# One of five score products contracts 128 rows instead of 64: the rotary keys' low halves in two zero-padded copies

## The chip, the cores and the metric

The kernel runs on one core of a Trainium2 chip. The metric is the device time of one execution in microseconds (us). Before the change it is 720.41 us, the median of 3 runs (720.25 to 720.73).

## The reference

One decoder layer over 512 tokens of width 1024: two parallel mixers with gates, an output projection, and a gated feed-forward with a causal convolution, all float32. The change touches the attention's scores alone. Each of 8 heads has 128 features without position and 64 turned by position (the rotary part); the rotary key is one for all heads:

```
k_rope = apply_rope(k_rope, cos, sin)                      # (tokens, 64), shared by the heads
s = einsum('bqhd,bkhd->bhqk', qn, k_nope) + einsum('bqhr,bkr->bhqk', qr, k_rope)
s = where(key_pos <= q_pos, s * scale, -inf)
p = softmax(s);  out = einsum('bhqk,bkhd->bqhd', p, v)     # queries in blocks of 128
```

## The kernel before

Every float32 value that enters a product is split in two: a high part H, rounded to the format float32r, and the rest, a low part L. A product of two such values is three matmuls, H·H, H·L and L·H, summed in one bank of PSUM (`mm3`, L79). ScalarE writes H (a cast), VectorE writes L (a subtraction): the helpers `split` (L75) and `wsplit` (L65), the latter for weights.

The layer runs in stages: the norm and the small projections; the spatial gate's values (two halves `hf`, four pairs of rows `pr`); the attention, head by head; the merging of the two mixers; the output projection; the feed-forward, which is the longest. In the loop over heads (L487) each turn does, on TensorE: the scores of head h, a gate's wide projection (`gate`, 24 products of 512 columns, the bank `pza`), the transposes of head h's probabilities (`turn`, L457), the query and key projections of head h + 1 (`qk`, in every second head also `rope`, which makes the next pair's turned queries), a second wide projection (`pzu` or `pzb`), and the sum over values (`attend`, the bank `po`).

The scores of one head are four blocks of 128 queries; block i sees (i + 1) · 128 keys, so the products have 128, 256, 384 and 512 columns. Each block is five matmuls (L434 to L438): three for the part without position, two for the rotary part. For the latter `rope` keeps the queries of a pair of heads so that one tile holds both parts: the head with e = 0 has its H in partitions 0 to 63 and its L in 64 to 127, the head with e = 1 the other way round. The keys stand twice, once in each half of the partitions: `krH` (high part) and `krL` (low part), [128, 512] each. L438 contracts all 128 rows with `krH`, which gives H·H + L·H at once. L437 contracts the 64 rows `own` in which the query's H lies, with `krL`. The keys are split once, at L323, in the stage of the spatial gate's values.

The softmax of a block is on VectorE and ScalarE: mask (L440), maximum (L441), exponential (L443), reciprocal (L445), scaling (L446). The transposes of block i read what L446 wrote for it. The work of heads 0 to 3 also carries a layer norm of the spatial gate's values (L521 to L531), mostly on VectorE.

A scheduler (the tile framework) sets the order on each engine from the order of the code and from priorities; the softmax has a high one. Engines take their instructions in that order. SP's queue issues the loads of weights ahead of their use into three rotating buffers.

Of the kernel before, what the change touches and what calls it, by code (L numbers as in the profile page):

```python
# [15 lines left out]
P = 128  # L16
D = 1024
S = 512
# [14 lines left out]

# columns of the packed per-feature parameters
PM, PQ, PFF, PCW, PCB, PFN = 0, 8, 11, 19, 151, 195
NPAR = 203
# columns of the packed constants
CI, CM, CF = 0, 128, 256
# [4 lines left out]
def block_kernel(ctx, tc, xT, pos, w_s, w_v, w_g, w_q, w_kv, w_o, w_u, w_d,  # L43
# [39 lines left out]

# [1 line left out]
    part = cp.tile([P, NPAR], F32, name="part")  # L85
# [4 lines left out]

    # the scalar engine's first table
    tb = cp.tile([P, 1], F32, name="tb")
# [18 lines left out]

    # keeps the tensor engine's clock up until the first operands are there
    pw = bank("warm")
# [3 lines left out]
    def col_mean(o, terms, c):  # L117
        """o [P, blocks]: by token, the sums over partitions of the terms, times column c of mcol."""
        for b in range(o.shape[1]):
            for a, t in enumerate(terms):  # L120
                T.matmul(o[:, b:b + 1], lhsT=t[:, b * P:(b + 1) * P], rhs=mcol[:, c:c + 1],
                         start=a == 0, stop=a == len(terms) - 1)
# [5 lines left out]
    def over_partitions(rt, pool, n, cols=NT):  # L128
        """A value by token, [P, cols], on all partitions: a bank [P, cols * P]."""
        dH = pool.tile([P, cols * P], F32R, tag="dH", name=f"dH_{n}", bufs=1)  # L130
        dL = pool.tile([P, cols * P], F32R, tag="dL", name=f"dL_{n}", bufs=1)
        for b in range(cols):
            c = slice(b * P, (b + 1) * P)
            A.mul(dH[:, c], ident, rt[:, b:b + 1])
            V.scalar_tensor_tensor(out=dL[:, c], in0=ident, scalar=rt[:, b:b + 1], in1=dH[:, c].bitcast(F32),
                                   op0=ALU.mult, op1=ALU.subtract)
        pb = bank(f"pb_{n}")
        T.matmul(pb[:, :cols * P], lhsT=ones, rhs=dH, start=True, stop=False)
        T.matmul(pb[:, :cols * P], lhsT=ones, rhs=dL, start=False, stop=True)
        return pb[:, :cols * P]  # L140
# [10 lines left out]
    def turned(t1, t2, z):  # L151
        """t1: z turned by its tokens' angles; 64 features after 64, a feature's partner 32 away."""
        V.tensor_tensor(out=t1, in0=z, in1=CC, op=ALU.mult)
        for q in range(4):
            a, b = slice(32 * q, 32 * q + 32), slice(32 * (q ^ 1), 32 * (q ^ 1) + 32)
            V.tensor_tensor(out=t2[a], in0=z[b], in1=SS[b], op=ALU.mult)
        V.tensor_tensor(out=t1, in0=t1, in1=t2, op=ALU.add)

# [1 line left out]
    hH = [None] * KC  # L160
# [12 lines left out]
    krH = mx.tile([P, S], F32R, name="krH")  # L173
    krL = mx.tile([P, S], F32R, name="krL")
    cqH = [mx.tile([P, S], F32R, name=f"cqH{i}") for i in range(2)]
# [5 lines left out]
    with tc.tile_pool(name="st", bufs=2) as st:  # L181
        # x, by chunks of features; the first weights behind each pair of them
        raws = []
# [40 lines left out]

        # rotary tables, by token, then turned: the cosines [c c c c], the sines [s -s s -s]
        ang = st.tile([P, P], F32, tag="ang", name="ang", bufs=1)
# [7 lines left out]
        def turns(o, t, unit):  # L234
            """Whole turns in t, to a multiple of the unit."""
            V.tensor_scalar(out=o, in0=t, scalar1=1.0 / (TWO_PI * unit), scalar2=MAGIC, op0=ALU.mult, op1=ALU.add)
            V.tensor_scalar(out=o, in0=o, scalar1=MAGIC, scalar2=unit, op0=ALU.subtract, op1=ALU.mult)
# [3 lines left out]

        # a turn in three parts, the first two short enough for exact products
        n8 = st.tile([P, P], F32, tag="n8", name="n8", bufs=1)
# [22 lines left out]

        # low-rank queries and keys, times their norms' gains; the squares without them
        pmx = bank("pm_x")
# [11 lines left out]

        # the spatial gate's values, by token: two halves of the features, four banks each
        for hf in range(2):
            pv = [bank(f"pv{hf}{t}") for t in range(NT)]
            for pr in range(4):
# [8 lines left out]
                if hf == 0 and pr == 0:  # L293
# [3 lines left out]
                    col_mean(pmq[:, NT:2 * NT], sqs[2:], 2)  # L297
                    # rstd_x * (mean(raw^2) * rstd_x^2 + eps)^-1/2
                    msq = st.tile([P, 2, NT], F32, tag="msq", name="msq", bufs=1)
# [5 lines left out]
                    inv_root(rtq.rearrange("p a t -> p (a t)"), msq.rearrange("p a t -> p (a t)"))  # L305
                    # the queries carry the scores' scale
                    for i in range(2):
# [10 lines left out]
                if hf == 0 and pr == 2:  # L318
                    V.tensor_tensor(out=cq[3], in0=cq[3], in1=rx, op=ALU.mult)
                    t1 = st.tile([P, S], F32, tag="t1", name="kt1", bufs=1)  # L320
                    t2 = st.tile([P, S], F32, tag="t2", name="kt2", bufs=1)
                    turned(t1, t2, cq[3])
                    split(krH, krL, t1)  # L323
                if hf == 1 and pr == 0:
# [13 lines left out]
    def gchunk(n, g):  # L338
        """One chunk of 128 of the wide projection's features, over all tokens."""
        raw = wtile(w_g[g], f"g{g}")  # L340
        wh, wl = wsplit(raw, f"g{g}")
        pz = bank(f"pz{n}{g}")
        for j in range(KC):
            c = slice(j * P, (j + 1) * P)
            mm3(pz, wh[:, c], wl[:, c], hH[j], hL[j], j == 0, j == KC - 1)
        return pz
# [19 lines left out]
    with tc.tile_pool(name="at", bufs=1) as at:  # L366
# [25 lines left out]
        def qproj(o, g, c0):  # L392
            """128 columns of a pair of heads' queries, from c0 of each half of the rows."""
            wh, wl = wqs[g]
            for k in range(2):
                c = slice(k * 384 + c0, k * 384 + c0 + P)
                mm3(o, wh[:, c], wl[:, c], cqH[k], cqL[k], k == 0, k == 1)

        def rope(g):
            """A pair of heads: the turned queries' parts, [H | L] of the one and [L | H] of the other."""  # L400
            pa = bank(f"ra{g}")
# [4 lines left out]
            for e in range(2):  # L406
# [3 lines left out]
                V.tensor_tensor(out=T_[oth], in0=t1[own], in1=T_[own].bitcast(F32), op=ALU.subtract)  # L410
                rT[2 * g + e] = (T_, own)

# [11 lines left out]
        def scores(h, qt):  # L424
            qH, qL, kH, kL = qt
            tq, own = rT[h]
            p_ = at.tile([P, 1280], F32, tag="p", name=f"p{h}")
            sm = at.tile([P, 3, 4], F32, tag="sm", name=f"sm{h}", bufs=2)
            pS = [bank(f"s{h}{i}") for i in range(NT)]
            for i in range(NT):  # L430
# [5 lines left out]
                T.matmul(o, lhsT=qL[:, qs], rhs=kH[:, :n], start=False, stop=False)  # L436
                T.matmul(o, lhsT=tq[own, qs], rhs=krL[own, :n], start=False, stop=False)  # L437
                T.matmul(o, lhsT=tq[:, qs], rhs=krH[:, :n], start=False, stop=True)  # L438
# [9 lines left out]

        # turned blocks: keys 0 | keys 1, keys 3 | keys 2
        place = {0: (0, 0), 1: (1, 0), 3: (1, 384), 2: (2, 0)}  # L450
# [36 lines left out]
        for h in range(H):  # L487
# [18 lines left out]
            if h == 0:  # L506
# [3 lines left out]
                                base=0, channel_multiplier=-1)  # L510
                # layer norm of the values; their gains and shifts lie where late chunks will
                gb = [uy.tile([P, S], F32, tag=f"u{4 + i}", name=f"gb{i}") for i in range(4)]
# [21 lines left out]
    with tc.tile_pool(name="mg", bufs=2) as mg:  # L534
# [17 lines left out]

        # output projection, the residual, and the next norm's squares
        x1t = [hp.tile([P, D], F32, tag=f"d{t}", name=f"x1_{t}") for t in range(NT)]
# [21 lines left out]

# [1 line left out]
    fp = ctx.enter_context(tc.tile_pool(name="fp", bufs=1))  # L578
# [14 lines left out]
    def conv(pz, f):  # L593
        """f: the chunk's place in the parameters; a causal convolution of width three."""
        z = f2.tile([P, S + 2], F32, tag="z", name=f"z{f}")
# [39 lines left out]
    for j in range(KC - 2):  # L635
# [13 lines left out]
        if j == 1:  # L649
            # the last two chunks' weights, where the normed residual was and behind it  # L650
            eh, el = [], []
# [21 lines left out]

    # the last two chunks: three blocks of tokens as before, then the fourth by token; its other
    # features are turned to it, so that only a quarter's norm is left behind the last product
    n = S - P
# [21 lines left out]
    for i in range(NF):  # L698
        mm3(pB[:, :256], aH[i][:, tB], aL[i][:, tB], eh[i], el[i], i == 0, i == NF - 1)
        if i == 1:  # L700
            # the residual, turned as it is added
            for k in range(2):
# [29 lines left out]
def _layout(x, positions, mix_norm, w_in, a_v_norm_g, a_v_norm_b, a_spatial_w, a_spatial_b, q_a_norm,  # L732
# [11 lines left out]
    def rows(m):  # L744
        # [pairs of 128 rows, partition, (which of the pair, column)]
        return m.reshape(4, 2, P, -1).transpose(0, 2, 1, 3).reshape(4, P, -1)

    def cols(m):
        # [128 columns, partition, (chunk of 128 rows, column)]
        k, n = m.shape  # L750
# [58 lines left out]
```

## Time and profile before

| | |
|---|---|
| median of 3 runs | 720.41 us |
| profiled execution, its span from first to last instruction | 720.1 us |
| busy: TensorE products / weight loads | 710.9 us / 587.8 us |
| busy: VectorE / ScalarE / GpSimd | 476.9 us / 331.6 us / 11.4 us |
| granted TensorE clock, mean | 0.998 |
| DMA, mean over the span | 97 GB/s |

The profile gives for the profiled execution its span alone; the 0.3 us between it and the median is all that can be said of what lies around it. PE is TensorE's stream of products, PEld its weight loads, DVE is VectorE, ACT ScalarE, POOL GpSimd. Starts of matmuls are recorded, their ends are modelled, and a product's recorded duration overlaps that of the next: the time that a product takes from the stream is the distance from its start to the next one's start. Transposes are float32 products with the identity.

### The profile page before, as it was taken

What the parts mean: (1) busy time and instruction counts of PE and PEld (TensorE: products, weight loads), DVE (VectorE), ACT (ScalarE), POOL (GpSimd) and SP (SyncE); (2) the same over time, 40 slices, a digit from 0 to 9 for tenths busy, and PEclk for the clock granted to TensorE, in tenths of its full rate; (3) what the DMA queues carried; (4) which work ended last, traced back from release to release, by engine and by line L of the source; (5) the groups of instructions that cost most, each with busy time, mean ns of one, the idle gap of its engine ahead of it and who ended that gap; (6) DMA issues with size and microseconds to landing.
All of it is one profiled execution on the core that took longest, in us unless ns stands there. A gap on an engine that the chain in (4) does not pass through costs nothing.

```text
span 720.1 us, 8624 instructions
## 1 busy us (share of the span) xinstructions
PE 710.9 (99%) x3303; PEld 587.8 (82%) x3303; DVE 476.9 (66%) x816; ACT 331.6 (46%) x496; POOL 11.4 (2%) x14
## 2 busy tenths in 40 slices
PE   8999999999999999999999999999999999999996
PEld 5888877788787888878888888888888888888896
DVE  7966799967668567765477777776777775432104
ACT  5465555774756543343354444444444444422101
POOL 0000110000000000000100000000000000000000
PEclk9999999999999999999999999999999999999999
DMA  7524422130111111252322232222223225631003
GB/s 248 177 76 142 162 81 80 59 111 30 58 61 58 60 59 58 95 198 90 111 93 88 89 112 93 89 102 103 88 93 112 85 83 162 189 102 52 0 1 117
DMA packets 22617, 69.63 MB, mean 97 GB/s; under 512 B 2736, under 2 KB 4400, under 8 KB 22576
## 3 DMA queue, kind: packets, MB, share of 16 engines
q1 hardware_dynamic: 21568, 66.72, 27.6%
q10 hardware_dynamic: 1008, 2.36, 0.9%
q8 instruction: 26, 0.43, 0.3%
q14 instruction: 15, 0.12, 0.1%
HBM read 66.97 MB, written 2.10 MB: 96 GB/s over the span
## 4 chain that ended last, share of the span: by engine, by line
PE 97%; DMA 1%; SPq 0%; ACT 0%; DVE 0%; issue 0%; POOLq 0%; DVEq 0%
PE pup L80 11%; PE pup L82 11%; PE pup L81 11%; PE pd L82 4%; PE pd L81 4%; PE pd L80 4%; PE pout L81 2%; PE pout L82 2%; PE pout L80 2%; PE pv L80 2%; PE pza L82 2%; PE pzb L80 2%; PE pzb L82 2%; PE pza L80 2%; PE pzu L81 2%; PE pza L81 2%
## 5 line engine op out<-in xcount | busy, mean ns | idle before, releaser
L70 ACT CAST wh_u<-wr_u 128x1024 fp32r<-128x1024 f32 x44 | 46.3, 1052 | 41.6 <-PE pup L81 29.5
L71 DVE TENSOR_TENSOR wl_u<-wr_u,wh_u 128x1024 fp32r<-128x1024 f32 x44 | 53.9, 1225 | 8.1 <-ACT wh_u L70 7.0
L598 DVE TENSOR_TENSOR z<-pup,r 128x512 f32<-128x512 f32 x44 | 30.2, 687 | 35.1 <-PE pup L82 35.1
L80 PE MATMUL pd<-aH,wh_d 128*128 128x512 f32 x132 | 51.3, 389 | 0.0
L81 PE MATMUL pd<-aL,wh_d 128*128 128x512 f32 x132 | 51.3, 389 | 0.0
L82 PE MATMUL pd<-aH,wl_d 128*128 128x512 f32 x132 | 51.3, 389 | 0.0
L70 ACT CAST wh_g<-wr_g 128x1024 fp32r<-128x1024 f32 x24 | 25.2, 1049 | 50.4 <-issue 29.9
L71 DVE TENSOR_TENSOR wl_d<-wr_d,wh_d 128x896 fp32r<-128x896 f32 (+1 forms) x18 | 20.4, 1136 | 29.5 <-ACT wh_d L70 29.2
L76 ACT CAST aH<-y 128x512 fp32r<-128x512 f32 x22 | 13.7, 621 | 56.7 <-DVE z L597 54.2
L70 ACT CAST wh_d<-wr_d 128x896 fp32r<-128x896 f32 (+1 forms) x18 | 17.7, 982 | 44.1 <-PE pd L81 36.1
L600 ACT ACTIVATE y<-z,part 128x512 f32<-128x512 f32 x44 | 35.9, 818 | 3.4 <-DVE z L598 1.8
L71 DVE TENSOR_TENSOR wl_g<-wr_g,wh_g 128x1024 fp32r<-128x1024 f32 x24 | 29.8, 1244 | 7.2 <-ACT wh_g L70 7.1
L604 DVE SCALAR_TENSOR_TENSOR y<-z,part,y 128x512 f32<-128x512 f32 x44 | 33.0, 751 | 1.4
L602 DVE SCALAR_TENSOR_TENSOR y<-z,part,y 128x512 f32<-128x512 f32 x44 | 32.8, 747 | 0.3 <-ACT y L600 0.3
L617 ACT ACTIVATE y<-y 128x512 f32<-128x512 f32 x22 | 13.9, 632 | 36.4 <-DVE y L604 36.4
L80 PEld LDWEIGHTS pd<-aH,wh_d 128*128 128x128 f32 x132 | 24.8, 188 | 5.2
L81 PEld LDWEIGHTS pd<-aL,wh_d 128*128 128x128 f32 x132 | 24.8, 188 | 5.2
L82 PEld LDWEIGHTS pd<-aH,wl_d 128*128 128x128 f32 x132 | 24.8, 188 | 5.1
L81 PE MATMUL pout<-mL,wh_o 128*128 128x512 f32 x64 | 25.4, 397 | 0.0
L82 PE MATMUL pout<-mH,wl_o 128*128 128x512 f32 x64 | 25.3, 395 | 0.0
L80 PE MATMUL pout<-mH,wh_o 128*128 128x512 f32 x64 | 25.2, 396 | 0.0
L77 DVE TENSOR_TENSOR aL<-y,aH 128x512 fp32r<-128x512 f32 x22 | 15.2, 693 | 14.2 <-ACT aH L76 14.2
(594 smaller groups left out, 2006.2 us busy)
## 6 DMA issues: line engine op xcount, KB each, us to landing
wr_u<-in_w_u_dram SPq DMA_DIRECT2D x44, 512.0 KB, 3.3
wr_g<-in_w_g_dram SPq DMA_DIRECT2D x24, 512.0 KB, 3.3
wr_d<-in_w_d_dram SPq DMA_DIRECT2D x12, 448.0 KB, 3.3
x<-in_xT_dram SPq DMA_DIRECT2D x16, 256.0 KB, 4.4
wr_v<-in_w_v_dram SPq DMA_DIRECT2D x8, 512.0 KB, 4.4
wr_o<-in_w_o_dram SPq DMA_DIRECT2D x8, 512.0 KB, 3.3
wr_d<-in_w_d_dram SPq DMA_DIRECT2D x6, 512.0 KB, 3.5
wr_e<-in_w_e_dram SPq DMA_DIRECT2D x5, 512.0 KB, 3.6
```

Of the source, the lines that this page charges most:

```text
L70: A.copy(th[:, lo:hi], raw[:, lo:hi])
L71: V.tensor_tensor(out=tl[:, lo:hi], in0=raw[:, lo:hi], in1=th[:, lo:hi].bitcast(F32), op=ALU.subtract)
L76: A.copy(th, src)
L77: V.tensor_tensor(out=tl, in0=src, in1=th.bitcast(F32), op=ALU.subtract)
L80: T.matmul(o, lhsT=wh, rhs=xh, start=start, stop=False)
L81: T.matmul(o, lhsT=wh, rhs=xl, start=False, stop=False)
L82: T.matmul(o, lhsT=wl, rhs=xh, start=False, stop=stop)
L598: V.tensor_tensor(out=z[:, 2:], in0=pz, in1=r2, op=ALU.mult)
L600: A.activation(out=y, in_=z[:, 2:], func=AF.Identity, scale=part[:, w + 2:w + 3], bias=part[:, PCB + f:PCB + f + 1])
L602: V.scalar_tensor_tensor(out=y, in0=z[:, 1:S + 1], scalar=part[:, w + 1:w + 2], in1=y, op0=ALU.mult, op1=ALU.add)
L604: V.scalar_tensor_tensor(out=y, in0=z[:, 0:S], scalar=part[:, w:w + 1], in1=y, op0=ALU.mult, op1=ALU.add)
L617: A.activation(out=yg, in_=yg, func=AF.Silu)
```

## The change

`krL` becomes two tiles. The copy of index e holds the low parts in the half of the partitions where a head of that parity keeps its query's H, and zeros in the other half. GpSimd fills the zeros, and VectorE makes the subtraction in two halves. L437 (now L443) contracts all 128 rows with the copy of its head's parity, as L438 (now L444) does with `krH`. The rest of the difference is comments that are gone, and the slice that the dictionary `rT` no longer carries.

```
-    krL = mx.tile([P, S], F32R, name="krL")
+    krL = [mx.tile([P, S], F32R, name=f"krL{e}") for e in range(2)]
...
-                    split(krH, krL, t1)
+
+                    A.copy(krH, t1)
+                    for e in range(2):
+                        own, oth = slice(e * 64, e * 64 + 64), slice(64 - e * 64, 128 - e * 64)
+                        G.memset(krL[e][oth].bitcast(F32), 0.0)
+                        V.tensor_tensor(out=krL[e][own], in0=t1[own], in1=krH[own].bitcast(F32),
+                                        op=ALU.subtract)
...
-                rT[2 * g + e] = (T_, own)
+                rT[2 * g + e] = T_
...
-            tq, own = rT[h]
+            tq = rT[h]
...
-                T.matmul(o, lhsT=tq[own, qs], rhs=krL[own, :n], start=False, stop=False)
+                T.matmul(o, lhsT=tq[:, qs], rhs=krL[h % 2][:, :n], start=False, stop=False)
```

On TensorE, in the scores of head 1 (s is the bank of a block's scores, qt the parts of queries and keys, rT the turned queries), before:

```order
L436 MATMUL s_1099<-qt_1008,qt_1007 128x128
L437 MATMUL s_1099<-krL,rT_784 128x128
L438 MATMUL s_1099<-krH,rT_784 128x128
L434 MATMUL s_1100<-qt_1008,qt_1006 128x256
L435 MATMUL s_1100<-qt_1009,qt_1006 128x256
```

and after the change at the same place:

```order
L442 MATMUL s_1103<-qt_1012,qt_1011 128x128
L443 MATMUL s_1103<-krL_106,rT_788 128x128
L444 MATMUL s_1103<-krH,rT_788 128x128
L440 MATMUL s_1104<-qt_1012,qt_1010 128x256
L441 MATMUL s_1104<-qt_1013,qt_1010 128x256
```

Nothing has moved there: the shape shown is that of the output, line numbers are six higher, and the product with krL reads the second copy, as head 1 is odd. The whole stream of TensorE is the same in this way.

On VectorE, in the stage of the spatial gate's values (kt is the turned key, wl the low part of a weight), before:

```order
L157 TENSOR_TENSOR kt_532<-kt_532,kt_533 128x512
L135 SCALAR_TENSOR_TENSOR dL_q<-cstt,rtq,dH_q 128x128 x2
L71 TENSOR_TENSOR wl_v_648<-wr_v_645,wh_v_647 128x1024
L77 TENSOR_TENSOR krL<-kt_532,krH 128x512
L521 BN_STATS bst_1085<-vA_112 128x6
```

and after:

```order
L157 TENSOR_TENSOR kt_533<-kt_533,kt_534 128x512
L135 SCALAR_TENSOR_TENSOR dL_q<-cstt,rtq,dH_q 128x128 x2
L71 TENSOR_TENSOR wl_v_652<-wr_v_649,wh_v_651 128x1024
L328 TENSOR_TENSOR krL_105<-kt_533,krH 64x512
L328 TENSOR_TENSOR krL_106<-kt_533,krH 64x512
L527 BN_STATS bst_1089<-vA_113 128x6
```

One instruction has become two, at the same place. On GpSimd the two fills (64x512 each) stand ahead of the first power of the norm, right behind the program's start; nothing else has moved on any engine.

## Rows read from the trace of the kernel before

**Rows 1.** The page: TensorE's busy share, and the chain that ended last, by engine

```profile
PE 710.9 (99%) x3303; PEld 587.8 (82%) x3303; DVE 476.9 (66%) x816; ACT 331.6 (46%) x496; POOL 11.4 (2%) x14
...
PE 97%; DMA 1%; SPq 0%; ACT 0%; DVE 0%; issue 0%; POOLq 0%; DVEq 0%
```

**Rows 2.** Groups by shape on TensorE: count, busy us, mean ns, idle before

```profile
L438 PE MATMUL s<-krH,rT 128*128 128x512 f32 x8 | 4.0, 500 | 0.0
L437 PE MATMUL s<-krL,rT 64*128 64x512 f32 x8 | 4.0, 499 | 0.0
```

**Rows 3.** Timeline of TensorE, scores of head 1: start us, duration us, what

```profile
115.42 0.28 PE L434 MATMUL s<-qt,qt 128*128 128x128 f32 x1
...
118.56 0.39 PE L434 MATMUL s<-qt,qt 128*128 128x512 f32 x1
...
119.02 0.40 PE L436 MATMUL s<-qt,qt 128*128 128x512 f32 x1
119.35 0.50 PE L437 MATMUL s<-krL,rT 64*128 64x512 f32 x1
119.78 0.50 PE L438 MATMUL s<-krH,rT 128*128 128x512 f32 x1
120.12 0.39 PE L80 MATMUL pza<-hH0a,wh_g 128*128 128x512 f32 x1
```

**Rows 4.** Timeline of TensorE, start and end of the last head's scores

```profile
246.34 0.28 PE L434 MATMUL s<-qt,qt 128*128 128x128 f32 x1
...
251.04 0.39 PE L80 MATMUL pza<-hH0a,wh_g 128*128 128x512 f32 x1
```

**Rows 5.** Timeline of TensorE, start of head 0's sum over values

```profile
113.55 0.39 PE L80 MATMUL po<-pH,vH 128*128 128x512 f32 x1
```

**Rows 6.** Busy us (and instructions) in three stretches, then clock, DMA share, GB/s

```profile
94.60:104.90 10.30, 10.30 (x46) 7.72 (x45) 10.23 (x28) 5.26 (x11) 0.93 (x1) 1.00 0.31 103
115.40:137.40 22.00, 22.00 (x107) 17.73 (x106) 19.61 (x42) 12.66 (x23) 0.90 (x1) 1.00 0.14 47
137.40:251.10 113.70, 113.70 (x543) 90.99 (x542) 79.45 (x162) 72.25 (x126) 0.00 (x0) 1.00 0.19 64
```

**Rows 7.** Timeline of TensorE, transposes of heads 0 and 1

```profile
104.92 1.25 PE L457 MATMUL pT<-cstt,p 128*128 128x128 f32 x10
105.93 0.47 PE L80 MATMUL pq<-cqH,wqH 128*128 128x512 f32 x1
...
125.58 1.25 PE L457 MATMUL pT<-cstt,p 128*128 128x128 f32 x10
```

**Rows 8.** Timeline of VectorE, softmax of heads 0 and 1 [idle before, releaser]

```profile
103.91 0.79 DVE L446 TENSOR_SCALAR p<-p,sm 128x384 f32<-128x384 f32 x2
...
120.31 0.30 DVE L440 TENSOR_TENSOR s<-s,cstt 128x128 f32<-128x128 f32 x1 [0.47 <-PE s L438]
...
122.90 1.06 DVE L446 TENSOR_SCALAR p<-p,sm 128x256 f32<-128x256 f32 x3
```

**Rows 9.** Timeline of VectorE, the keys' split and two splits of weights

```profile
51.16 1.22 DVE L71 TENSOR_TENSOR wl_v<-wr_v,wh_v 128x1024 fp32r<-128x1024 f32 x1
52.30 0.68 DVE L77 TENSOR_TENSOR krL<-kt,krH 128x512 fp32r<-128x512 f32 x1
53.75 0.69 DVE L521 BATCH_NORM_STATS2 bst<-vA 128x6 f32<-128x512 f32 x1 [0.77 <-ACT vA L331]
...
73.57 1.72 DVE L71 TENSOR_TENSOR wl_g<-wr_g,wh_g 128x1024 fp32r<-128x1024 f32 x1 [4.17 <-ACT wh_g L70]
```

**Rows 10.** Groups by shape on VectorE: the split of the turned queries

```profile
L410 DVE TENSOR_TENSOR rT<-t,rT 64x512 fp32r<-64x512 f32 x8 | 5.5, 686 | 0.3
```

**Rows 11.** Timeline of GpSimd: a fill, the first power, the select

```profile
0.41 0.10 POOL L795 MEMSET const-uint8-127<- 128x1 uint8 x1
30.45 1.39 POOL L126 TENSOR_TENSOR rtx<-msx,mhalf 128x4 f32<-128x4 f32 x1 [29.95 <-DVE msx L125]
...
73.11 1.10 POOL L509 TENSOR_SCALAR_AFFINE_SELECT wst<-wst 128x1024 f32<-128x1024 f32 x1 [33.43 <-DMA wst<-in_ws_t_dram]
```

## The prediction

> **What bounds the kernel now.** I read the page's busy shares first, then the chain that ended last. TensorE is busy for 710.9 of 720.1 us and the chain runs over it for 97% [rows 1], so any time taken out of TensorE's own stream is a candidate for the whole kernel, unless another engine is late right there. The second view is that of the changed line's matmuls by shape: the 64-row product with krL (L437) lasts 499 ns at 512 columns, and the 128-row product with krH behind it 500 ns [rows 2]. Half the rows are no shorter. But ends of matmuls are modelled, so the third view decides: the order of starts on TensorE in one head.
>
> Read the starts of the last block of queries in head 1 [rows 3]. From L434 to L436 are two products in 119.02 − 118.56 = 0.46, that is 0.23 us for one of 512 columns. Then L436 to L437 takes 0.33, L437 to L438 0.43, and L438 to the next product 0.34. The three distances around the 64-row product are 0.10, 0.20 and 0.11 longer than the standard 0.23. The same rows give the whole of a head: the first score product starts at 115.42 and the first one after the scores at 120.12, so the 20 products (four widths, five of each) take 4.70 us. The last head shows the same, 251.04 − 246.34 = 4.70 [rows 4]. There is no idle time in these rows: the array passes from 128 rows to 64 and back to 128, and pays around that passage.
>
> What would the 20 products take with no such passage? The kernel itself holds the answer: just before these scores the attention output runs three products of each of the same four widths, all of 128 rows, from 113.55 to the first score product at 115.42 [rows 3, 5]: 1.87 us for twelve, 0.62 us for one of each width. Five of each make 5 × 0.62 = 3.12 us. So the passages cost 4.70 − 3.12 = 1.58 us in each head.
>
> **The change part by part.** (1) The krL product takes all 128 rows, with zeros opposite the query's half that must not count. Its columns stay the same, and columns are what a product's distance goes by: 0.23 for 512, 0.62 for the four widths. It reads the same stationary tile as the krH product behind it. I take the full-height product at the price of any other, and the passages are gone: 1.58 us from each of eight heads, 12.6 us on TensorE. The bounds: nothing, if what I call a passage belongs to something that stays, and 12.6.
>
> The Trainium skill, "TensorEngine Tiling (Array Packing)", section "Theoretical Speedup", speaks against padding: a contraction of 64 rows or fewer can go up to twice as fast when the array is split in rows. By that rule the half-height product was cheap and the full one adds a whole product to every block; by the rows above the time falls. The trace does not bear the rule out here, since nothing runs beside L437: its successor starts 0.43 us later, not earlier than the standard 0.23. What such a rule would give here is worked out as the last rival.
>
> (2) What of the 12.6 us reaches the end. TensorE must not run into work of VectorE that is not ready, so I looked at both in each head. In the stretch of head 0 up to its transposes VectorE is busy for 10.23 of 10.30 us [rows 6]: it follows a backlog, and nothing in it waits for TensorE, so an earlier TensorE does not make it earlier. The last scaled probabilities of head 0 (L446, two instructions shown as one) end there at 103.91 + 0.79 = 104.70; ten transposes start at 104.92 and the next product at 105.93 [rows 7, 8], so one takes 0.10 and the four that need the last block start at 104.92 + 0.60 = 105.52. They could start 0.82 us earlier, less some 0.05 for the hand-over. Head 0 thus gives about 0.77 of its 1.58 us, and waits for the rest.
>
> In head 1 VectorE still has the backlog, but it idles 0.47 us at 120.31 for that head's last scores [rows 8], which will come 0.77 + 1.58 = 2.35 us earlier; so it moves up 0.47 us. Its last probabilities then end at 122.90 + 1.06 − 0.47 = 123.49. The transposes that need them stood at 125.58 + 0.60 = 126.18 [rows 7] and move to 123.83. They keep 0.3 us, so head 1 gives all its 1.58; should the margin be gone, the loss is a few tenths. From 115.4 to 137.4 VectorE has 22.00 − 19.61 = 2.4 us to spare, and behind that it is busy for 79 of 113.7 us [rows 6], so that the six later heads give all. The sum is 0.77 + 7 × 1.58 = 11.8 us.
>
> (3) The order on TensorE is unchanged, product for product; so no bank of PSUM, weight tile or DMA on SP's queue has a new predecessor.
>
> (4) Split of the keys' low half: VectorE's one instruction of 0.68 us at 52.30 becomes two with half the partitions and the same columns. Such an instruction, that of the queries' parts, takes 686 ns [rows 10]: 0.69 us more. Behind it VectorE idles 0.77 us for ScalarE before it can go on at 53.75 [rows 9], which covers it. Without that cover it would be 0.69 us on VectorE in a stage where TensorE waits for nothing, and the waits before the backlog of head 0 would take it up.
>
> (5) Two fills with zeros, 64 x 512, on GpSimd, which now stand first in its program. The trace has no such fill; it lies between the 0.10 us of a fill of one column and the 1.10 us of the select over 128 x 1024 [rows 11], as an estimate at most 2.2 us for both. They start near 0.5 us; GpSimd's next work is at 30.45 [rows 11], and the first reader is in head 0, past 94.6. Can they hold up VectorE? A split on VectorE at 73.57, beside the select, took 1.72 us, and one of the same shape at 51.16 took 1.22 [rows 9, 11] (I read the difference as the select's doing); so a fill could cost VectorE's first constants some tenths, at most its own 1.1 us. TensorE then runs its warming products until the first weights and features, so I take nothing, and keep 0 to 1 us in the range.
>
> The terms that reach the end are −11.8 (1 and 2), 0 (3), 0 (4) and 0 (5). Against the profiled execution's own span, 720.1 us, that gives 708.3; the median of the runs shown is 0.3 above that span, which I keep for what lies around it: 708.6 us.
>
> **The rivals.**
> VectorE's backlog eats more. Heads 0 to 2 give nothing because VectorE, nearly full in 94.6 to 115.4, does not catch up: the gain is 5 × 1.58 = 7.9 us, 712.5. For it speaks 10.23 of 10.30 busy; against it the 0.47 us of idle in head 1 and the 2.4 us in the stretch behind.
>
> It does not do what it says. The long distances belong to the turned queries, whose same tile is loaded as weights twice in a row, and not to the rows: then nothing is gained and 720.4 stays. Against it: L434 and L435 read one stationary tile (qH) as well, and the distance from the one to the other and on to L436 is the standard 0.23.
>
> The half-height product was the cheap one. If the number of rows sets a product's time, the 128-row product costs a full share more, and the distances above 0.23 stay. The place is the eight heads' TensorE stream, which nothing covers; the price is one product of each width, 0.62 us a head, 8 × 0.62 = 5.0 us, 725.4. It decides if L443 of the changed kernel keeps the 0.43 and more that L437 shows. Against it stands that 499 and 500 ns are equal, and that the distance before L437, where only a 128-row product ends, is long already.
>
> **How the numbers follow.** My forecast (10 to 12.6 us less) has 0.82, the backlog rival (6 to 10 us less) 0.10, no effect 0.05, slower 0.03. The time is 708.6. The range reaches from 707.4, where all 12.6 us come through and 0.4 is left for spread, to 711.2: head 0 giving nothing (0.8), head 1 half (0.8), and 1 us for the fills. It leaves out most of the backlog rival and the last two. A change within 0.2%, 1.4 us, can't be told from none with this kernel: that is the case of no effect. Faster 0.92, same 0.05, slower 0.03.
>
> **What would show it.** In the profile after: all five score products of a block 0.23 us apart at 512 columns, and eight stretches of scores of about 3.1 us instead of 4.7; a wait of TensorE of under 1 us for the scaled probabilities in head 0, at the transposes, and none or a trace of one in head 1; VectorE's two half splits near 52 with no wait of TensorE behind them; the fills done by 3 us. I am wrong if L443 or L444 keeps a distance over 0.3, or if the waits at the transposes go on through heads 2 and 3.

## The result and the profile after

The changed kernel takes 709.86 us (median of 4 runs, 708.88 to 710.90) against 720.57 us before (4 runs, 720.25 to 720.83): a ratio of 0.9852 with a 95% interval from 0.9838 to 0.9866. It is faster by 10.7 us, inside the predicted range and 1.3 us above the predicted 708.6 us.

The page of the profile after answers to [rows 1]; TensorE is as full as before, but 11.3 us shorter, and the chain that ended last now lies on VectorE for 3%, in the stretch that ends at head 0's transposes:

```profile
span 707.6 us, 8629 instructions
PE 699.6 (99%) x3303; PEld 586.6 (83%) x3303; DVE 476.5 (67%) x817; ACT 331.5 (47%) x496; POOL 12.3 (2%) x16
PE 94%; DVE 3%; DMA 2%; issue 0%; ACT 0%; SPq 0%; POOLq 0%; DVEq 0%
```

The groups by shape on TensorE (count, busy us, mean ns, idle before) answer to [rows 2]:

```profile
L444 PE MATMUL s<-krH,rT 128*128 128x512 f32 x8 | 3.1, 393 | 0.0
L443 PE MATMUL s<-krL,rT 128*128 128x512 f32 x8 | 3.1, 387 | 0.0
```

Both products of 512 columns have lost about 110 ns of recorded duration, the 64-row one and the 128-row one behind it. What that is worth is in the timeline of the scores of head 1 (start us, duration, what), which answers to [rows 3]:

```profile
113.23 0.28 PE L440 MATMUL s<-qt,qt 128*128 128x128 f32 x1
...
113.79 0.33 PE L440 MATMUL s<-qt,qt 128*128 128x256 f32 x1
...
115.31 0.39 PE L440 MATMUL s<-qt,qt 128*128 128x512 f32 x1
...
115.77 0.40 PE L442 MATMUL s<-qt,qt 128*128 128x512 f32 x1
116.01 0.39 PE L443 MATMUL s<-krL,rT 128*128 128x512 f32 x1
116.23 0.39 PE L444 MATMUL s<-krH,rT 128*128 128x512 f32 x1
116.46 0.39 PE L80 MATMUL pza<-hH0a,wh_g 128*128 128x512 f32 x1
```

The distances around L443 are 0.24, 0.22 and 0.23 us, where they were 0.33, 0.43 and 0.34. The scores of a head take 116.46 − 113.23 = 3.23 us instead of 4.70.

The weight loads of the same block show where the time lay. TensorE's loads before (start us, duration, what, [idle before, releaser], where "issue" stands for a wait for nothing that the profile shows):

```profile
118.79 0.19 PEld L436 LDWEIGHTS s<-qt,qt 128*128 128x128 f32 x1
119.34 0.18 PEld L437 LDWEIGHTS s<-krL,rT 64*128 64x128 f32 x1 [0.37 <-issue]
119.77 0.19 PEld L438 LDWEIGHTS s<-krH,rT 128*128 128x128 f32 x1 [0.25 <-issue]
```

and after:

```profile
115.77 0.19 PEld L443 LDWEIGHTS s<-krL,rT 128*128 128x128 f32 x1
```

Between products of 128 rows a load starts ahead of its product, with the product before it: at 118.79 for L436's product at 119.02, and after the change at 115.77 for L443's product at 116.01. Where the number of rows changed, it started together with its own product, at 119.34 and 119.77 for the products at 119.35 and 119.78. Why the load is not started ahead there, no run shows.

The last head (starts on TensorE, as in [rows 4]) shows 238.49 − 235.26 = 3.23 again:

```profile
235.26 0.28 PE L440 MATMUL s<-qt,qt 128*128 128x128 f32 x1
...
238.49 0.39 PE L80 MATMUL pza<-hH0a,wh_g 128*128 128x512 f32 x1
```

Heads 0 and 1 at the transposes, on TensorE and on VectorE, answer to [rows 7, 8]:

```profile
102.28 1.71 PE L463 MATMUL pT<-cstt,p 128*128 128x128 f32 x10
103.74 0.47 PE L80 MATMUL pq<-cqH,wqH 128*128 128x512 f32 x1
...
121.92 1.25 PE L463 MATMUL pT<-cstt,p 128*128 128x128 f32 x10
122.93 0.47 PE L80 MATMUL ra<-cqH,wqH 128*128 128x512 f32 x1
```

```profile
102.48 0.80 DVE L452 TENSOR_SCALAR p<-p,sm 128x384 f32<-128x384 f32 x2
```

In head 0 the transposes start 0.50 us behind the product ahead of them (101.78), where it was 0.23, and the ten take 1.46 us from the stream instead of 1.01, because the last block is scaled only at 103.28; in head 1 they take 1.01 again. Head 0's scores started on TensorE, before and after, at

```profile
94.80 0.22 PE L434 MATMUL s<-qt,qt 128*128 128x128 f32 x1
```

```profile
93.38 0.22 PE L440 MATMUL s<-qt,qt 128*128 128x128 f32 x1
```

From there to the first score product of head 1 were 115.42 − 94.80 = 20.62 us and are now 113.23 − 93.38 = 19.85 us, 0.77 less; each later head gave between 1.46 and 1.50.

### The profile page after: what moved, and what is told of

Read it like the earlier page. It is cut to its first block, busy times and chain, and to the rows that moved or that the text cites. A ratio compares the mean times of both kernels' runs of the same rounds, so it can differ in the third digit from the quotient of the medians.

```text
span 707.6 us, 8629 instructions
## 1 busy us (share of the span) xinstructions
PE 699.6 (99%) x3303; PEld 586.6 (83%) x3303; DVE 476.5 (67%) x817; ACT 331.5 (47%) x496; POOL 12.3 (2%) x16
## 4 chain that ended last, share of the span: by engine, by line
PE 94%; DVE 3%; DMA 2%; issue 0%; ACT 0%; SPq 0%; POOLq 0%; DVEq 0%
PE pup L81 11%; PE pup L82 11%; PE pup L80 11%; PE pd L81 4%; PE pd L80 4%; PE pd L82 4%; PE pout L81 2%; PE pout L80 2%; PE pout L82 2%; PE pzb L82 2%; PE pzb L80 2%; PE pzb L81 2%; PE pv L80 2%; PE pv L82 2%; PE pza L81 2%; PE pv L81 2%
## 5 line engine op out<-in xcount | busy, mean ns | idle before, releaser
L80 PE MATMUL pd<-aH,wh_d 128*128 128x512 f32 x132 | 51.3, 389 | 0.0
L80 PEld LDWEIGHTS pd<-aH,wh_d 128*128 128x128 f32 x132 | 24.8, 188 | 5.2
L80 PE MATMUL pout<-mH,wh_o 128*128 128x512 f32 x64 | 25.2, 396 | 0.0
```

Of the source, the lines that this page charges most:

```text
L80: T.matmul(o, lhsT=wh, rhs=xh, start=start, stop=False)
```

## The experiments

All times are medians of the runs named, but for the second profile of the kernel before, which is one run; the runs of the kernel before on the same chip stand beside them. The changed kernel was run again beside most of them.

**The changed kernel again.**

> The changed kernel itself, for more runs and a second profile. In the first profile the first score product of head 0 starts at 93.38 us, 1.42 earlier than before the change, though nothing ahead of it should be faster; the eight heads then give 0.77 + 7 x 1.47 = 11.1 us. If the 1.42 us is chance of the first transfers, it comes and goes between profiles, and the mean gain stays between 10 and 12 us. If the fills on GpSimd or another part of the change moved the start for good, head 0 starts at 93.4 again. Scores of a head: 3.23 us.

709.28 us (5 runs, 708.64 to 710.17) against 720.79 us, ratio 0.9844 (0.9831 to 0.9858). Head 0 starts at 93.39, as in the first profile and as in the profiles below whose start is that of the kernel before; so the 1.42 us ahead of head 0 were not the change's doing. Unexpected was that head 0 now gives 20.62 − 19.14 = 1.48 us and not 0.77. On VectorE the profiles part at one wait, ahead of the layer norm's second multiplication. The timeline of VectorE [idle before, releaser], in the first profile after the change and in this one:

```profile
79.32 0.75 DVE L536 SCALAR_TENSOR_TENSOR vA<-vA,rv,gb 128x512 f32<-128x512 f32 x1 [1.54 <-DMA gb<-in_vb_dram]
```

```profile
78.00 0.75 DVE L536 SCALAR_TENSOR_TENSOR vA<-vA,rv,gb 128x512 f32<-128x512 f32 x1 [0.35 <-DMA gb<-in_vb_dram]
```

All that VectorE does between there and the probabilities of head 0 moves with it: the last scaling starts at 102.48 in the one and at 101.15 in the other. And this time the transposes take 1.00 us:

```profile
102.03 1.25 PE L463 MATMUL pT<-cstt,p 128*128 128x128 f32 x10
103.03 0.47 PE L80 MATMUL pq<-cqH,wqH 128*128 128x512 f32 x1
```

**Half as many passages, with the same products.** The 64-row products of neighbouring blocks are put side by side:

```
+                odd = i % 2 == 1
+                if odd:
+                    T.matmul(o, lhsT=tq[own, qs], rhs=krL[own, :n], start=True, stop=False)
...
-                T.matmul(o, lhsT=tq[own, qs], rhs=krL[own, :n], start=False, stop=False)
-                T.matmul(o, lhsT=tq[:, qs], rhs=krH[:, :n], start=False, stop=True)
+                T.matmul(o, lhsT=tq[:, qs], rhs=krH[:, :n], start=False, stop=odd)
+                if not odd:
+                    T.matmul(o, lhsT=tq[own, qs], rhs=krL[own, :n], start=False, stop=True)
```

> The kernel before with the same 64-row products, ordered so that those of blocks 0 and 1, and those of blocks 2 and 3, stand next to each other: the array goes from 128 to 64 rows and back twice in a head instead of four times. Theory (the cost is the passage): half of the 1.47 us a head goes, 0.73 x 8 = 5.9 us, about 714.6 us, scores of a head 3.9 to 4.0 us. Rival (each 64-row product carries the cost itself, wherever it stands): 4.70 us a head and 720.5 us, as before.

715.59 us (4 runs, 714.54 to 716.56) against 720.79 us, ratio 0.9926 (0.9913 to 0.9940): 5.2 us less, where 5.9 were expected. The timeline of TensorE in head 1 shows one such pair, and the end of the scores:

```profile
113.28 0.28 PE L437 MATMUL s<-qt,qt 128*128 128x128 f32 x1
...
115.35 0.34 PE L440 MATMUL s<-krH,rT 128*128 128x384 f32 x1
115.61 0.44 PE L442 MATMUL s<-krL,rT 64*128 64x384 f32 x1
115.89 0.39 PE L436 MATMUL s<-krL,rT 64*128 64x512 f32 x1
116.22 0.50 PE L437 MATMUL s<-qt,qt 128*128 128x512 f32 x1
116.56 0.39 PE L438 MATMUL s<-qt,qt 128*128 128x512 f32 x1
...
117.25 0.39 PE L80 MATMUL pza<-hH0a,wh_g 128*128 128x512 f32 x1
```

A head takes 3.97 us, 0.73 less than 4.70. The kernel has the same 64-row products as before the change, so the cost does not go with their number.

**One passage there and back in a head.** All four 64-row products first:

```
+            for i in range(NT):
+                n = (i + 1) * P
+                T.matmul(pS[i][:, :n], lhsT=tq[own, i * P:n], rhs=krL[own, :n], start=True, stop=False)
             for i in range(NT):
...
-                T.matmul(o, lhsT=tq[own, qs], rhs=krL[own, :n], start=False, stop=False)
```

> The kernel before with the four 64-row products of a head at the front of its scores, one behind the other: one passage there and back in a head. Theory (the cost is the passage): three quarters of 1.47 go, scores of a head about 3.6 us, the gain 8 x 1.1 less some 0.3 that head 0 waits for VectorE: 712.1 us. Rival (each 64-row product carries the cost itself): 4.70 us a head, 720.5 us.

711.75 us (4 runs, 711.32 to 714.05), ratio 0.9880 (0.9865 to 0.9894): 9.0 us less. The timeline of TensorE in head 1:

```profile
112.75 0.28 PE L82 MATMUL po<-pH,vL 128*128 128x128 f32 x1
112.96 0.90 PE L432 MATMUL s<-krL,rT 64*128 64x128 f32 x4
113.79 0.33 PE L437 MATMUL s<-qt,qt 128*128 128x128 f32 x1
...
116.44 0.39 PE L80 MATMUL pza<-hH0a,wh_g 128*128 128x512 f32 x1
```

3.48 us a head, from its first score product on. But here the scores begin with the 64-row products, so the way into the stretch lies ahead of that start: the last product of the sum over values is 112.96 − 112.75 = 0.21 us ahead, where it is 0.11 before a product of 128 rows (113.12 to 113.23 in the changed kernel). With these 0.10 us the head takes 3.58. From head 1 to head 2 the distance says the same, 20.92 us against 20.57 in the changed kernel. So with four, two, one and no stretches of 64 rows a head's scores take 4.70, 3.97, 3.58 and 3.23 us: 0.37 us for each stretch, there and back, and 0.35 us for the single one with four products in it.

**Two 64-row products in each block.** The rotary product with krH is cut to the query's high part, which leaves out the query's low part against krH:

```
-                T.matmul(o, lhsT=tq[:, qs], rhs=krH[:, :n], start=False, stop=True)
+                T.matmul(o, lhsT=tq[own, qs], rhs=krH[own, :n], start=False, stop=True)
```

> The kernel before with both rotary products on the 64 rows of the query's high part, so that the query's low part against krH is left out: as many products and as many columns, as many passages, but two 64-row products side by side in each block. Theory (the cost is the passage): 4.70 us a head and 720.5 us, as before. Rival (each 64-row product costs more by itself, 0.43 us at 512 columns against 0.34 for its successor): 0.09 us for each of 32 blocks, 2.9 us, 723.4 us. Rival (rows set the time, a half-height product is cheap): below 720, by up to half of 5.0 us.

720.73 us (10 runs) against 720.79 us, ratio 0.9998 (0.9989 to 1.0007). Twice the 64-row products cost nothing more and save nothing. The scores of a head take 4.59 us in the profile against 4.70, but the missing 0.1 us only falls behind their end: the first product of the gate is now the first of 128 rows, and it takes 118.84 − 118.51 = 0.33 us instead of 0.23. From head to head the distances are those of before (22.05 and 22.04 us from head 1 to head 2). The rows of the last block show that the long distance behind L437 is gone, 0.34 instead of 0.43, since its successor is of 64 rows too (its load starts at 117.96, ahead of its product again), and that the passage back lies behind L438 and behind L80:

```profile
117.52 0.40 PE L436 MATMUL s<-qt,qt 128*128 128x512 f32 x1
117.85 0.49 PE L437 MATMUL s<-krL,rT 64*128 64x512 f32 x1
118.19 0.39 PE L438 MATMUL s<-krH,rT 64*128 64x512 f32 x1
118.51 0.50 PE L80 MATMUL pza<-hH0a,wh_g 128*128 128x512 f32 x1
118.84 0.40 PE L81 MATMUL pza<-hL0a,wh_g 128*128 128x512 f32 x1
```

With these three runs the rivals fall in which the half-height product is cheap or carries the cost by itself.

**What head 0 gives: the loads of the norm's gains first.** The loads of wst and bsb are moved from h == 0 to h == 4 in the code, so that gb is loaded ahead of them.

> The changed kernel, with the four loads of the layer norm's gains and shifts (gb) ahead of those of the spatial weights and shifts (wst, bsb), which are not needed before the merging stage. In two profiles of the changed kernel VectorE waits 1.54 and 0.35 us for gb at the head of the backlog of head 0, and head 0 gives 0.77 and 1.48 us. Theory (what head 0 loses hangs on the landing of gb alone): no wait of VectorE for gb, the transposes of head 0 wait for nothing, head 0 to head 1 takes 19.1 us instead of 19.85, and the kernel is 0 to 0.7 us below the changed one: 708.6 to 709.3 us. Rival (VectorE's amount of work is the limit whenever gb lands): head 0 to head 1 stays at 19.8 us.

709.81 us (5 runs, 708.75 to 710.02) against 709.18 us of the changed kernel beside it: no gain, and the expectation failed. The wait for gb is gone, but another one took its place. GpSimd's select over wst now runs late and stands ahead of the power that the norm needs. The timelines of GpSimd and of VectorE:

```profile
77.26 1.67 POOL L521 TENSOR_SCALAR_AFFINE_SELECT wst<-wst 128x1024 f32<-128x1024 f32 x1 [38.64 <-DMA bsb<-in_bs_dram]
78.90 0.55 POOL L532 TENSOR_TENSOR rv<-rv,mhalf 128x1 f32<-128x1 f32 x1
```

```profile
79.48 0.75 DVE L537 SCALAR_TENSOR_TENSOR vA<-vA,rv,gb 128x512 f32<-128x512 f32 x1 [1.51 <-POOL rv L532]
```

Head 0 to head 1 took 19.67 us.

**The changed kernel beside it.**

> The changed kernel, beside the others on the same chip: 709 to 710 us; scores of a head 3.23 us; the first score product at 93.4 us, or 1.4 us later where the first weights land late.

709.18 us (4 runs, 708.30 to 710.08), ratio 0.9839. VectorE waited 1.22 us for gb and passed the multiplication at 79.17; head 0 to head 1 took 19.80 us.

**No fills on GpSimd.** `G.memset(...)` becomes `V.tensor_scalar(out=krL[e][oth], in0=t1[oth], scalar1=0.0, scalar2=None, op0=ALU.mult)`.

> The changed kernel with the zeros written by VectorE (the turned key times 0) next to the split, and no fill on GpSimd at the start. Theory (the fills cost nothing): the same time as the changed kernel within 0.5 us, VectorE's cast of ones at 1.40 us back to 0.23 us from 0.57, and two instructions more on VectorE near 50 us with nobody waiting. Rival (the fills hold up the start): the first score product earlier by some tenths.

710.68 us (4 runs, 708.92 to 710.95) against 709.18 (708.30 to 710.08): not faster, with ranges that overlap, and 1.5 us above it where 0.5 was expected. In its profile VectorE waited 2.30 us for gb and passed the multiplication at 80.78, and head 0 to head 1 took 20.62 us; the first score product came at 94.07, not earlier. So the fills do not hold up the start. Nor do the two more instructions on VectorE make the profile late: TensorE is 0.73 us behind the first profile of the changed kernel at 12.19 us already, long before the zeros are written (50.27), and 0.69 us behind at the first score product; and at the second split of a weight behind them (56.00) VectorE too is 0.69 us behind and no more, since it waits there 1.45 us for ScalarE instead of 2.28. gb's last loads are issued 0.7 us later, and why they take longer still to land is not shown.

**The kernel before, a second profile.**

> The kernel before once more, for a second profile. In its first profile TensorE waits 1.4 us for the first weights at 12.5 us and the first score product starts at 94.80; in five profiles of other kernels with the same start it starts at 93.3 to 93.4. If that wait is chance: 93.4 here, a span near 718.7, and scores of 4.70 us a head.

721.40 us (one run), a span of 719.7, the first score product at 93.49, and scores of 4.70 us. The early wait of the first profile was chance. But head 0 to head 1 now takes 21.50 us instead of 20.62: even before the change the transposes of head 0 waited for VectorE when gb landed late:

```profile
81.08 0.75 DVE L530 SCALAR_TENSOR_TENSOR vA<-vA,rv,gb 128x512 f32<-128x512 f32 x1 [1.21 <-DMA gb<-in_vb_dram]
```

**The norm's multiplications behind head 0.** gb goes to tiles that a first column from head 0's sum over values holds back (`A.copy(gb[2 * i + k][:, :1], yB[0][:, :1])` ahead of each load, tags y4 to y7), and the code of the norm moves one head down, its last block excepted, which stays in head 3.

> The changed kernel with the layer norm's multiplications moved behind head 0: its gains and shifts are loaded into tiles that become free only behind head 0's sum over values (their first column is written from it before the load), so that no instruction of VectorE ahead of head 0's softmax waits for that load or for GpSimd's power. In the changed kernel's profiles so far head 0 to head 1 takes 19.14 to 19.85 us by how long VectorE waited for gb. Theory (an in-order wait of VectorE for gb sets what head 0 gives): 19.1 us whenever gb lands, no wait at the transposes of head 0, and 0 to 0.7 us below the changed kernel, 708.6 to 709.2 us. Rival (the later heads have no room for the norm on VectorE): TensorE waits at the transposes of heads 2 to 4 and the kernel is not faster than the changed one.

711.67 us (4 runs, 710.81 to 712.80) against 708.53 us of the changed kernel beside it: slower by 3.1 us. Head 0 does give all it has (19.13 us). The loss is in head 2, where the scores take 5.66 us: VectorE now does the norm's work ahead of the turned queries. The timeline of TensorE in head 2 [idle before, releaser]:

```profile
133.63 0.33 PE L441 MATMUL s<-qt,qt 128*128 128x128 f32 x1 [0.38 <-DVE qt L77]
133.80 0.28 PE L442 MATMUL s<-qt,qt 128*128 128x128 f32 x1
135.67 0.33 PE L443 MATMUL s<-krL,rT 128*128 128x128 f32 x1 [1.59 <-DVE rT L416]
```

The rival held: the later heads had no room, at the turned queries and not, as I had written it, at the transposes.

**The changed kernel beside it.**

> The changed kernel on the same chip as the one above: 709 to 710 us, head 0 to head 1 between 19.1 and 19.9 us.

708.53 us (4 runs, 708.21 to 709.29), ratio 0.9832; a wait of 0.33 us for gb, the multiplication at 78.16, head 0 to head 1 in 19.13 us.

**Gains first, and the select out of the way.** The first column of wst is written from yB[0] before its load, so that load and select come behind head 0; gb is loaded first as above.

> The changed kernel with the gains and shifts (gb) loaded first, and the load of the spatial weights and the select over them on GpSimd held back behind head 0, so that neither the load nor GpSimd stands in front of the layer norm; the order of VectorE in heads 0 and 1 is that of the changed kernel. Theory (what head 0 gives hangs on when VectorE can go on with the norm, not on the amount of its work): VectorE passes the norm's second multiplication before 78.1 us, head 0 to head 1 takes 19.1 us, and the eight heads give 11.8 us: 708.3 to 709.0 us. Rival (the work itself is too much in some executions): transposes of head 0 wait although nothing of VectorE waited for gb or GpSimd.

709.09 us (5 runs, 708.39 to 709.28) against 708.54 us of the changed kernel beside it. The mechanism is as expected: VectorE waits for nothing ahead of the multiplication and passes it at 77.96, and head 0 to head 1 takes 19.13 us.

```profile
76.64 1.41 DVE L536 SCALAR_TENSOR_TENSOR vA<-vA,mv,gb 128x512 f32<-128x512 f32 x2
77.96 0.75 DVE L538 SCALAR_TENSOR_TENSOR vA<-vA,rv,gb 128x512 f32<-128x512 f32 x1
```

The time is 0.1 us above the expected range, and not below the changed kernel's, which passed the multiplication almost as early here:

> The changed kernel on the same chip: 708.4 to 709.9 us; head 0 to head 1 at 19.1 us if VectorE waits less than 0.5 us for gb, up to 19.9 us if it waits 1.5 us.

708.54 us (4 runs, 708.12 to 709.93), ratio 0.9833 (0.9819 to 0.9846); a wait of 0.44 us for gb, the multiplication at 78.12, head 0 to head 1 in 19.14 us. No version that I tried beats the changed kernel.

Over all eight profiles without 64-row products in which the norm stands ahead of head 0 one rule holds. In four of them the transposes waited: the multiplication at 79.32, 79.17, 79.48 and 80.78, and head 1's first product at 113.23, 113.10, 113.39 and 114.69. The distance is 33.91, 33.93, 33.91 and 33.91 us: VectorE's instructions from there to head 0's probabilities, and TensorE's from the transposes on, are one unbroken chain. In the other four (78.00, 78.12, 77.96 and 78.16) VectorE's part ends too early to matter, and TensorE's own 19.13 to 19.14 us counts. The second profile of the kernel before fits too, with 81.08 and 114.99.

## Why the prediction was right, and where its sizes were off

**The passages (1).** The step is shown. It was read from the distances and not from the recorded durations, and that was what mattered: 499 and 500 ns look alike in [rows 2], though the cost lay in both. The size was off: predicted 4.70 − 3.12 = 1.58 us a head, measured 1.47. The error is the 3.12. It came from the sum over values, whose widths go down [rows 3, 5], times five thirds. In the scores the widths go up, and five products of 128 columns take 113.79 − 113.23 = 0.56 us, 0.11 each, where a third of that sum's share for 128 columns, 115.42 − 115.14 = 0.28, gives 0.09: the first of them had come only 0.06 before the second. That makes 0.09 of the 0.11 us. Eight heads hold 11.8 us, not 12.6. The rival that the turned queries' tile, loaded twice in a row, carries the cost falls with the rows after: L443 and L444 still load the same part of rT one behind the other, and their distance is 0.22 us.

**Head 0 (2).** The forecast of 0.77 us met the first profile to the hundredth, and that was luck, since I had only half of the reason. I wrote that VectorE's backlog fixes the time of head 0's probabilities and that TensorE cannot move it. That is right. But I took the backlog's place for fixed, and it hangs on the landing of gb: head 0 gives 0.77 us in one execution and 1.48 in another, and the kernel before loses there too, 0.88 us in its second profile. The wait was in the trace of before, 1.53 us ahead of the backlog, in a row that I did not show (VectorE):

```profile
80.76 0.75 DVE L530 SCALAR_TENSOR_TENSOR vA<-vA,rv,gb 128x512 f32<-128x512 f32 x1 [1.53 <-DMA gb<-in_vb_dram]
```

In the first profile after the change it happened to be the same, 1.54 us; where it was 0.35, head 0 gave 1.48. Head 1 gave all, as predicted, and so did heads 2 to 7; the rival of the backlog eating heads 0 to 2 is refuted by the changed kernel itself.

**The base.** I added 0.3 us to the span for what lies around it. The runs whose span is known show 1.7 to 1.9 (709.26 with a span of 707.6, 709.07 with 707.2). The first profile of before was of an execution about 1.4 us longer than most, with the wait at 12.5 us. So its 720.1 did not belong to the median of 720.41. This did not move the forecast, which came out as that median less 11.8. With 11.1 us for the heads (0.77 + 7 × 1.47) from a median of 720.57, the step gives 709.5 us; measured were 709.86 at first and 708.53 to 709.28 in four more sets. That two of these (708.53 and 708.54) come out at the 708.6 of the forecast is luck: in their profiles head 0 gave 1.49 and 1.48 us, more than I had counted, and the other heads less.

**The split (4) and the fills (5).** Two half splits take 1.38 us where one took 0.68, and VectorE goes on without idling, where it idled 0.77 us before [rows 9]:

```profile
50.88 1.38 DVE L328 TENSOR_TENSOR krL<-kt,krH 64x512 fp32r<-64x512 f32 x2
52.33 0.69 DVE L527 BATCH_NORM_STATS2 bst<-vA 128x6 f32<-128x512 f32 x1
```

So the cover that I named is what hid it. The two fills take 1.09 us together, within the bounds of [rows 11], and one of VectorE's first instructions does get longer beside them, 0.57 us instead of 0.23 (and 0.23 again where VectorE wrote the zeros), on GpSimd and VectorE:

```profile
0.79 1.09 POOL L327 MEMSET krL<- 64x512 f32 x2 [0.29 <-POOLq L801]
```

```profile
1.40 0.57 DVE L101 CAST ones<-one 128x128 fp32r<-128x128 f32 x1
```

VectorE has nothing to do then until 3.69, so it costs nothing, as taken.

**The cheap half-height product.** The section "Theoretical Speedup" of the Trainium skill's "TensorEngine Tiling (Array Packing)" promises up to twice the speed for contractions of 64 rows or fewer when the array is split. Nothing here shows it: two 64-row products in a row on the same rows took 0.34 and 0.32 us at 512 columns, no less than a full product (0.23) each, and the passages. Two products on different halves were not run together.

## What to carry to other kernels

A product on 64 of the array's 128 rows was no cheaper in a stream of full ones, and each stretch of them cost the way there and back, 0.35 to 0.37 us here (other heights were not run): pad with zeros where the other half can be zero, or gather such products into one stretch. Read it from the distance between starts of neighbouring products, never from their durations. When TensorE gets shorter, look on the other engines for the instruction at the head of an unbroken in-order chain that ends at TensorE: what releases that one, a load that lands early or late, decides what the saving is worth there.

## What was not expected of the hardware

The cost of a stretch of 64 rows hardly depends on how many products stand in it: four in a row added 0.35 us to a head, pairs 0.37 us each, single ones 0.37 us each. And the landing of two small loads, 256 KB each, varied enough between executions of one kernel to hold VectorE for 0.33 to 1.54 us; that alone moved the distance from head 0 to head 1 by 0.7 us.
